# Reordering the opening of an encoder layer: memory keys in the large PSUM tiles, statistics spread later, x^T loads interleaved with weights

## The chip, the cores and the metric

The kernel runs on one core of a Trainium2 chip. The metric is the device time of one execution in microseconds (us). TensorE (PE) multiplies, VectorE (DVE), ScalarE (ACT) and GpSimd (POOL) work on tiles in SBUF or PSUM, and the queue of SyncE (SP) issues the DMA transfers of this kernel, one after another.

## The reference

One encoder layer is applied to two request groups with shared weights: a prompt of 1024 tokens and a sample of 512, each with 256 memory tokens, all of width 1024. Cut to what matters here:

```
h  = rms_norm(x, ln_pre);  z = h @ w_in            # projections and gates of three branches
kv = rms_norm(mem, ln_mem) @ w_mem_kv              # memory keys (512 wide) and values (512 wide)
pool, self-attention, cross-attention into mk/mv
merged = sum_n sigmoid(gate_n) * (branch_n @ w_branch[n])
y = x + rms_norm(merged @ w_out, ln_post)
```

The change touches only the opening: the norms of the memory and of the prompt, and the memory's keys and values.

## The kernel before, in words

Everything is float32 at the interface. A product is made of three float32r matmuls (`mm3`, lines 139 to 142, issued at L133): each operand is split into a high part (ACT copies with rounding, L172) and a low part (DVE subtracts, L169), and hi*hi + hi*lo + lo*hi is summed in PSUM. The split of a 128x1024 weight tile is in `weights` (lines 181 to 188). Weights use three raw buffers (`RAW`) and two split buffers (`WT`), so a third weight can be loaded only when a raw buffer is free, and split only when the matmuls of the weight two before it are done.

The opening is `mem_phase` (lines 661 to 723) with `long_h` (lines 237 to 286) run beside it: `mem_phase` calls `next(others)` at chosen points, and each call runs `long_h` up to its next `yield`.

`mem_phase` loads the memory transposed (`mt`, both groups side by side, 512 columns) in four pieces and the first two key weights, splits the memory with its gain (L675 on ACT, L676 on DVE), and then runs four key stages (c = 0 to 3, 24 matmuls each, one bank of 512 columns in a small PSUM tile `B`) and four value stages (kk = 0 to 3, 24 matmuls each, in the four banks of the two large PSUM tiles `A`). The memory's norm is applied to the keys when a bank is evacuated (L700, then a split into `hu` tiles and four DMAs to scratch, L705) and to the values as a per-partition scale (L719, L720).

A norm takes this path: squares on ACT (L209) and two adds on DVE (L210, L211), `mean_squares` (16 small matmuls against `ones`, two columns wide, then an ACT copy at L204), `rstd_of` on POOL (L192, L196), and `spread`: DVE makes four diagonal blocks (L218), one float32 matmul against `ones` turns them into a 128x512 tile of the factors. Before the change the memory's path stands behind key stage 0 and the spread ahead of key stage 1.

`long_h` does the same for x^T of the prompt, in two halves of tokens j = 0, 1: four loads of 1 MB each, then per half the norm, then `scaled` (L258) multiplies by gain and factor, and the differences (L266) and `put` (splits at L172 and L169) make seven operands h[0] to h[6] for `products`, which forms each pair of weight tiles with seven half-size products instead of eight. Product i needs h[i]. `products` follows on the value stages, so the first one starts when these are done and h[0] is ready.

The instruction order of every engine is fixed when the kernel is built: the framework's scheduler orders by readiness in its own model of time and by priority, which is program order, moved ahead by AHEAD = 120 for weight splits and by EVAC = 200 for evacuations. An engine then waits at an instruction until its inputs are there.

Of the kernel before, what the change touches and what calls it, by code (L numbers as in the profile page):

```python
# [13 lines left out]
AF = mybir.ActivationFunctionType  # L14
# [4 lines left out]
P = 128  # L19
# [42 lines left out]
def encoder_kernel(ctx: ExitStack, tc, wt, xs, xts, mt, cols, rows, rope, edge, ys):  # L62
# [34 lines left out]
    def S(n):  # L97
        return st.tile([P, n], F32, tag=f"s{n}", bufs=3 if n == 16 else 8, name=nm("s"))
# [46 lines left out]
    def load(out, src):  # L145
        return nc.sync.dma_start(out, src)
# [24 lines left out]
    def split(hi, lo, x):  # L171
        act.activation(hi, x, AF.Copy)  # L172
        lo_of(lo, x, hi)
# [4 lines left out]
    def SUM():  # L178
        return sb.tile([P, D], F32, tag="sum", bufs=2, name=nm("sum"))

    def weights(*key):

        raw = RAW()
        load(raw[:], wt[TILES[key]])
        hi, lo = WT()
        with tc.high_priority(AHEAD):
            split(hi[:], lo[:], raw[:])
        return lambda s: (hi[:, s], lo[:, s])

    def rstd_of(ss):  # L190

        pool.tensor_scalar(ss, ss, EPS, 1.0, op0=ALU.add, op1=ALU.mult)  # L192
        n = ss.free_size()
        for i in range(0, n, 4):
            j = slice(i, min(i + 4, n))
            pool.tensor_tensor(ss[:, j], ss[:, j], mhalf[:, :j.stop - i], op=ALU.pow)  # L196
# [40 lines left out]
    def long_h(xt, h):  # L237

        h += [[None] * 4 for _ in range(7)]
        xv = xt.rearrange("p (k t) -> p k t", k=KC)  # L240
        q = [[M(F32) for _ in range(2)] for _ in range(2)]
        for j in range(2):
            for i in range(2):
                load(q[i][j][:].rearrange("p (c n) -> p c n", c=4), xv[:, i * 4:i * 4 + 4, j * BLK:(j + 1) * BLK])
        yield
        r, sp = S(16), []
        for j in range(2):
            rj = r[:, j * TT:(j + 1) * TT]
            mean_squares([squares(q[i][j][:]) for i in range(2)], rj)
            rstd_of(rj)  # L250
            sp.append(spread(rj))
            yield
        b11, b12, b21, b22 = [[q[i][j][:, :D], q[i][j][:, D:]] for i in range(2) for j in range(2)]

        def scaled(i, j):
            for c in range(4):
                x = q[i][j][:, c * BLK:(c + 1) * BLK]
                v.scalar_tensor_tensor(x, x, colt[:, i * 4 + c:i * 4 + c + 1], sp[j], op0=ALU.mult, op1=ALU.mult)  # L258

        def put(k, x):  # L260
            for c in range(2):
                parts_of(h[k], 2 * c, x[c])

        def difference(out, a, b):
            for c in range(2):
                v.tensor_tensor(out[c], a[c], b[c], op=ALU.subtract)  # L266

        scaled(0, 0)
        put(0, b11)
        yield  # L270
        scaled(1, 0)
        put(1, b21)
        yield
        scaled(0, 1)
        scaled(1, 1)
        yield
        t3, t4 = (U(), U()), (U(), U())
        difference(t3, b22, b12)
        difference(b12, b12, b11)
        difference(b11, b22, b12)  # L280
        put(2, b11)
        put(3, b12)
        put(4, t3)
        put(5, b22)
        difference(t4, b21, b11)
        put(6, t4)
# [374 lines left out]
    def mem_phase(mkd, mvd, others):  # L661

        raw, mh, ml = [M(F32) for _ in range(2)], [], []
        ws = []
        for i in range(4):
            load(raw[i // 2][:, i % 2 * D:(i % 2 + 1) * D], mt[:, i * D:(i + 1) * D])
            if i < 2:
                ws.append(weights("mk", i))
        for i in range(4):
            x = raw[i // 2][:, i % 2 * D:(i % 2 + 1) * D]  # L670
            hi, lo = sb.tile([P, 1024], F32R, tag="kt", bufs=4, name=nm("mh")), U(F32R)
            for k in range(2):
                s = slice(k * BLK, (k + 1) * BLK)
                g = colt[:, 8 + 2 * i + k:9 + 2 * i + k]
                act.activation(hi[:, s], x[:, s], AF.Copy, scale=g)  # L675
                v.scalar_tensor_tensor(lo[:, s], x[:, s], g, hi[:, s].bitcast(F32), op0=ALU.mult, op1=ALU.subtract)  # L676
                mh.append(hi[:, s])
                ml.append(lo[:, s])
        next(others)
        yield  # L680
        m = list(zip(mh, ml))
        r, sp = S(16), HU()

        def rstd():
            mean_squares([squares(raw[i][:]) for i in range(2)], r[:, :TT])
            rstd_of(r[:, :TT])
            spread(r[:, :TT], sp[:])

        for c in range(4):
            b, w = B(), ws.pop(0) if ws else weights("mk", c)  # L690
            for k in range(KC):
                mm3(b[:], w(slice(k * P, (k + 1) * P)), m[k], k == 0, k == KC - 1)
            if c == 0:
                rstd()
            else:
                next(others, None)
            yield
            t, hi, lo = HU(), HU(F32R), HU(F32R)
            with tc.high_priority(EVAC):
                v.tensor_tensor(t[:], b[:], sp[:], op=ALU.mult)  # L700
                split(hi[:], lo[:], t[:])
            for g in range(2):
                for s, x in enumerate((hi, lo)):
                    o = s * D + c * NMEM
                    nc.sync.dma_start(mkd[g][:, o:o + NMEM], x[:, g * NMEM:(g + 1) * NMEM].bitcast(F32))  # L705
        b = [a[:, i * BLK:(i + 1) * BLK] for a in (A(), A()) for i in range(2)]
        for kk in range(4):
            w = weights("mv", kk)
            for i in range(2):
                k = kk * 2 + i  # L710
                for t in range(TT):
                    ts = slice(t * P, (t + 1) * P)
                    mm3(b[t], (m[k][0][:, ts], m[k][1][:, ts]), w(slice(i * 512, (i + 1) * 512)), k == 0, k == KC - 1)
            next(others, None)
            yield
        for t in range(TT):
            hi, lo = HU(F32R), HU(F32R)
            with tc.high_priority(EVAC):
                act.activation(hi[:], b[t], AF.Copy, scale=r[:, t:t + 1])  # L719
                v.scalar_tensor_tensor(lo[:], b[t], r[:, t:t + 1], hi[:].bitcast(F32), op0=ALU.mult, op1=ALU.subtract)  # L720
            for s, x in enumerate((hi, lo)):
                o = s * D + t % 2 * BLK
                nc.sync.dma_start(mvd[t // 2][:, o:o + BLK], x[:].bitcast(F32))
# [289 lines left out]
                nc.sync.dma_start(dst[t * P:(t + 1) * P, n], x[:, n])  # L1013


    load(colt[:], cols)
    v.tensor_scalar_mul(hbias[:], colt[:, 16:40], 0.5)
    mkd, mvd = [[scratch(f"{n}_{g}", [P, 2 * D]) for g in range(2)] for n in ("mk", "mv")]
    h, hs = [], []
    ops = long_h(xts[1], h)  # L1020
    run(mem_phase(mkd, mvd, ops))
    run(ops)
    late_constants()
    sc, kt, vt, pairs, bg, tasks, drained = group(1)
    pre = short_h(xts[0], hs)
# [114 lines left out]
```

## Time and profile before

| | us |
|---|---|
| median of 3 runs | 1512.16 (1507.26 to 1512.44) |
| the profiled execution, its own time | 1511.38 |
| its span, first to last instruction | 1509.6 |
| PE busy in the span | 1462.9 (97%) |
| DVE busy | 981.2 (65%) |
| ACT busy | 709.2 (47%) |
| mean granted TensorE clock | 0.99 of full |

The span is 1.8 us shorter than the profiled execution's time, which lies 0.8 us under the median. "Busy" is time in which an engine executes; the bracket at the end of a timeline row is the idle time of that engine just before it and what ended it.

### The profile page before, as it was taken

What the parts mean: (1) busy time and instruction counts of PE and PEld (TensorE: products, weight loads), DVE (VectorE), ACT (ScalarE), POOL (GpSimd) and SP (SyncE); (2) the same over time, 40 slices, a digit from 0 to 9 for tenths busy, and PEclk for the clock granted to TensorE, in tenths of its full rate; (3) what the DMA queues carried; (4) which work ended last, traced back from release to release, by engine and by line L of the source; (5) the groups of instructions that cost most, each with busy time, mean ns of one, the idle gap of its engine ahead of it and who ended that gap; (6) DMA issues with size and microseconds to landing.
All of it is one profiled execution on the core that took longest, in us unless ns stands there. A gap on an engine that the chain in (4) does not pass through costs nothing.

```text
span 1509.6 us, 19658 instructions
## 1 busy us (share of the span) xinstructions
PE 1462.9 (97%) x7264; PEld 1207.9 (80%) x7264; DVE 981.2 (65%) x1262; ACT 709.2 (47%) x1097; POOL 272.4 (18%) x286
## 2 busy tenths in 40 slices
PE   5999999999999999999999999999989999999998
PEld 3778888888888888887888888888767878888887
DVE  5896586666648564646676676666667664764754
ACT  5354444544434544434565555666666323323332
POOL 0001020110000000301222222233233150150241
PEclk8999999999999999999999999999999999999999
DMA  7333234332323433344322222265326854954952
GB/s 274 100 112 110 84 112 126 106 132 65 127 91 93 155 119 126 112 138 138 91 65 78 96 65 90 81 213 185 126 72 233 313 179 138 338 192 141 337 163 84
DMA packets 88174, 211.37 MB, mean 140 GB/s; under 512 B 9872, under 2 KB 19216, under 8 KB 87312
## 3 DMA queue, kind: packets, MB, share of 16 engines
q1 hardware_dynamic: 88080, 210.14, 42.1%
q8 instruction: 57, 0.93, 0.3%
q14 instruction: 37, 0.30, 0.1%
HBM read 155.57 MB, written 54.53 MB: 139 GB/s over the span
## 4 chain that ended last, share of the span: by engine, by line
PE 83%; issue 4%; ACT 4%; DVE 4%; DMA 2%; POOL 1%; SPq 0%; DVEq 0%; POOLq 0%; ACTq 0%
PE B L133 65%; PE A L133 13%; PE A L137 5%; ACT u L769 1%; DMA hu<-xq 1%; DVE wlo L169 1%; ACT med L172 1%; ACT whi L172 1%; DVE s L767 1%; PE B L137 1%; DMA hu<-merge 1%; POOL med L925 1%; POOL s L196 0%; DVE med L169 0%; DMA med<-q 0%
## 5 line engine op out<-in xcount | busy, mean ns | idle before, releaser
L133 PE MATMUL B<-med,whi 128*128 128x512 f32 x2776 | 870.3, 393 | 1.1 <-ACT hu L359 1.1
L133 PEld LDWEIGHTS B<-med,whi 128*128 128x128 f32 x2776 | 513.5, 188 | 104.5 <-ACT hu L359 2.3
L133 PE MATMUL B<-med,wlo 128*128 128x512 f32 x1388 | 542.6, 391 | 0.7 <-DVE wlo L169 0.7
L172 ACT ACTIVATE whi<-raw 128x1024 fp32r<-128x1024 f32 (+1 forms) x168 | 167.3, 996 | 304.4 <-PE B L133 212.6
L133 PEld LDWEIGHTS B<-med,wlo 128*128 128x128 f32 x1388 | 260.7, 188 | 55.9 <-DVE wlo L169 1.7
L169 DVE TENSOR_TENSOR wlo<-raw,whi 128x1024 fp32r<-128x1024 f32 (+1 forms) x168 | 213.0, 1268 | 139.3 <-ACT whi L172 136.8
L172 ACT ACTIVATE med<-A 128x1024 fp32r<-128x1024 f32 (+1 forms) x108 | 96.9, 897 | 121.3 <-PE A L137 121.1
L771 POOL TENSOR_SCALAR u<-u,s 128x1024 f32<-128x1024 f32 (+1 forms) x96 | 94.6, 985 | 317.0 <-DVE s L770 275.7
L169 DVE TENSOR_TENSOR med<-A,med 128x1024 fp32r<-128x1024 f32 (+1 forms) x109 | 115.7, 1061 | 51.6 <-ACT med L172 50.0
L767 DVE TENSOR_REDUCE s<-A 128x1 f32<-128x1024 f32 (+1 forms) x96 | 100.1, 1043 | 42.7 <-PE A L133 20.8
L192 POOL TENSOR_SCALAR s<-s 128x16 f32<-128x16 f32 (+3 forms) x17 | 6.6, 388 | 671.8 <-DVE s L557 324.6
L769 ACT ACTIVATE u<-A,s 128x1024 f32<-128x1024 f32 (+1 forms) x96 | 93.1, 970 | 46.3 <-DVE s L767 45.8
L137 PE MATMUL A<-ident,u 128*128 128x128 f32 x784 | 107.2, 275 | 4.6 <-DVE med L169 2.1
L137 PEld LDWEIGHTS A<-ident,u 128*128 128x128 f32 x784 | 90.8, 141 | 24.8 <-issue 9.6
L133 PE MATMUL A<-kt,med 128*128 128x512 f32 x320 | 96.5, 415 | 10.0 <-ACT u L769 8.8
L925 POOL TENSOR_TENSOR med<-med,hu 128x512 f32<-128x512 f32 x48 | 77.4, 1625 | 136.1 <-DVE hu L923 136.1
L133 PE MATMUL A<-whi,med 128*128 128x512 f32 (+1 forms) x320 | 92.4, 368 | 0.2 <-ACT hu L954 0.2
L172 ACT ACTIVATE whi<-sum 128x1024 fp32r<-128x1024 f32 x50 | 53.1, 1062 | 64.3 <-PE B L133 62.1
L133 PEld LDWEIGHTS A<-kt,med 128*128 128x128 f32 x320 | 54.4, 190 | 34.2 <-ACT u L769 22.9
L133 PE MATMUL B<-med,vt 128*128 128x256 f32 x512 | 76.1, 288 | 1.4 <-ACT med L172 1.4
L169 DVE TENSOR_TENSOR med<-med,med 128x1024 fp32r<-128x1024 f32 (+1 forms) x50 | 55.5, 1115 | 33.7 <-ACT med L172 29.9
L172 ACT ACTIVATE med<-med 128x1024 fp32r<-128x1024 f32 (+1 forms) x44 | 44.3, 1019 | 68.8 <-POOL med L925 42.6
(173 smaller groups left out, 1567.2 us busy)
## 6 DMA issues: line engine op xcount, KB each, us to landing
raw<-wt SPq DMA_DIRECT2D x168, 512.0 KB, 3.7
merge<-hu SPq DMA_DIRECT2D x72, 256.0 KB, 2.1
hu<-merge SPq DMA_DIRECT2D x72, 256.0 KB, 5.4
med<-br SPq DMA_DIRECT2D x36, 256.0 KB, 5.2
q<-hu SPq DMA_DIRECT2D x24, 256.0 KB, 2.6
br<-hu SPq DMA_DIRECT2D x24, 256.0 KB, 2.5
med<-q SPq DMA_DIRECT2D x12, 512.0 KB, 4.5
med<-xt_prompt SPq DMA_DIRECT2D x4, 1024.0 KB, 13.2
```

The costliest lines, as they stand in the source:

```text
L133: pe.matmul(out, l, r, **k)
L137: pe.transpose(out, x, i[:])
L169: v.tensor_tensor(out, x, hi.bitcast(F32), op=ALU.subtract)
L172: act.activation(hi, x, AF.Copy)
L192: pool.tensor_scalar(ss, ss, EPS, 1.0, op0=ALU.add, op1=ALU.mult)
L767: v.reduce_max(mx[:], a[:, :L], axis=AX.X, negate=True)
L769: act.activation(p[:, :L], a[:, :L], AF.Exp, bias=mx[:], accum_out=sm[:])
L771: pool.tensor_scalar(p[:, :L], p[:, :L], rc[:], 1.0, op0=ALU.mult, op1=ALU.mult)
L925: pool.tensor_tensor(at, at, sg[:], op=ALU.add)
```

## The change

It makes these edits, all in the opening:

- A first ACT instruction copies one column of a constant, so that the activation table is loaded there. The constants `colt` are loaded behind the first piece of the memory instead of ahead of it, and `hbias` is made from them after the opening instead of at the start.
- The first key weight is split in two halves.
- The x^T loads are issued one at a time, with the third and the fourth key weight between them.
- The four key stages write the four banks of two `A` tiles instead of four `B` tiles.
- The memory's mean squares come after key stage 1, its spread after key stage 2. Stages 0 to 2 are evacuated after that spread, stage 3 after its own matmuls. The squares of half 0 of x come after stage 2, its spread after stage 3, the squares of half 1 after value stage 0, its spread (with `scaled` and `put` for h[0]) after value stage 1. The differences come after the value stages.

```diff
-    def weights(*key):
+    def weights(*key, pieces=1):
...
         with tc.high_priority(AHEAD):
-            split(hi[:], lo[:], raw[:])
+            for i in range(pieces):
+                s = slice(i * D // pieces, (i + 1) * D // pieces)
+                split(hi[:, s], lo[:, s], raw[:, s])
...
                 load(q[i][j][:].rearrange("p (c n) -> p c n", c=4), xv[:, i * 4:i * 4 + 4, j * BLK:(j + 1) * BLK])
-        yield
+                yield
...
             rstd_of(rj)
+            yield
             sp.append(spread(rj))
-            yield
+            if j == 0:
+                yield
...
             load(raw[i // 2][:, i % 2 * D:(i % 2 + 1) * D], mt[:, i * D:(i + 1) * D])
+            if i == 0:
+                load(colt[:], cols)
             if i < 2:
-                ws.append(weights("mk", i))
+                ws.append(weights("mk", i, pieces=2 - i))
...
         next(others)
-        yield
+        ws.append(weights("mk", 2))
+        next(others)
+        ws.append(weights("mk", 3))
+        next(others)
+        next(others)
         m = list(zip(mh, ml))
         r, sp = S(16), HU()
-
-        def rstd():
-            mean_squares([squares(raw[i][:]) for i in range(2)], r[:, :TT])
-            rstd_of(r[:, :TT])
-            spread(r[:, :TT], sp[:])
-
-        for c in range(4):
-            b, w = B(), ws.pop(0) if ws else weights("mk", c)
-            for k in range(KC):
-                mm3(b[:], w(slice(k * P, (k + 1) * P)), m[k], k == 0, k == KC - 1)
-            if c == 0:
-                rstd()
-            else:
-                next(others, None)
-            yield
+        b = [a[:, i * BLK:(i + 1) * BLK] for a in (A(), A()) for i in range(2)]
+
+        def evacuate(c):
             t, hi, lo = HU(), HU(F32R), HU(F32R)
             with tc.high_priority(EVAC):
-                v.tensor_tensor(t[:], b[:], sp[:], op=ALU.mult)
+                v.tensor_tensor(t[:], b[c], sp[:], op=ALU.mult)
                 split(hi[:], lo[:], t[:])
...
+        for c in range(4):
+            for k in range(KC):
+                mm3(b[c], ws[c](slice(k * P, (k + 1) * P)), m[k], k == 0, k == KC - 1)
+            if c == 1:
+                mean_squares([squares(raw[i][:]) for i in range(2)], r[:, :TT])
+                rstd_of(r[:, :TT])
+            elif c == 2:
+                spread(r[:, :TT], sp[:])
+                for i in range(3):
+                    evacuate(i)
+                next(others)
+            elif c == 3:
+                next(others)
+                evacuate(3)
+            yield
...
-    load(colt[:], cols)
-    v.tensor_scalar_mul(hbias[:], colt[:, 16:40], 0.5)
+    act.activation(mhalf[:, :1], mhalf[:, 1:2], AF.Copy)
...
     run(mem_phase(mkd, mvd, ops))
     run(ops)
+    v.tensor_scalar_mul(hbias[:], colt[:, 16:40], 0.5)
```

## Rows read from the trace of the kernel before

**Rows 1.** Long stretches: us, busy of PE, PEld, DVE, ACT, POOL, clock, DMA share, GB/s.

```profile
0.00:90.00 90.00, 69.42 (x280) 54.17 (x281) 68.24 (x84) 43.57 (x48) 5.40 (x12) 0.89 0.55 185
90.00:110.00 20.00, 18.86 (x87) 14.42 (x86) 18.33 (x22) 10.78 (x15) 0.00 (x0) 1.00 0.26 81
110.00:200.00 90.00, 90.00 (x420) 74.08 (x419) 60.41 (x88) 37.23 (x55) 11.45 (x11) 1.00 0.27 86
```

**Rows 2.** The same view of the opening, cut at its stages.

```profile
7.50:17.20 9.70, 8.48 (x24) 5.87 (x24) 9.33 (x13) 9.70 (x12) 0.00 (x0) 1.00 1.04 399
17.20:21.40 4.20, 2.28 (x16) 2.14 (x16) 3.72 (x5) 3.80 (x3) 0.00 (x0) 0.94 1.05 387
21.40:28.60 7.20, 0.08 (x2) 0.04 (x1) 2.87 (x4) 4.31 (x4) 2.20 (x2) 0.50 0.91 325
28.60:37.80 9.20, 9.20 (x26) 6.75 (x27) 4.86 (x7) 1.63 (x3) 0.00 (x0) 0.68 0.27 95
...
42.20:51.50 9.30, 9.30 (x27) 6.74 (x28) 6.71 (x9) 2.12 (x2) 0.00 (x0) 0.68 0.36 86
...
62.30:82.40 20.10, 20.10 (x89) 16.53 (x88) 19.63 (x23) 6.89 (x8) 0.00 (x0) 1.00 0.44 127
82.40:104.00 21.60, 20.46 (x89) 15.85 (x89) 21.06 (x24) 15.15 (x19) 0.00 (x0) 1.00 0.35 126
sum 104.00, PE 82.28 PEld 63.74 DVE 81.89 ACT 51.12 POOL 5.40; mean PE 7.48 PEld 5.79 DVE 7.44 ACT 4.65 POOL 0.49
```

**Rows 3.** Timeline of PE, opening: start, us, line, what [idle before <-releaser].

```profile
28.56 2.08 PE L133 MATMUL B<-u,ones 128*128 128x512 f32 x2 [7.12 <-DVE u L218]
37.84 1.84 PE L133 MATMUL B<-ones,hu 128*128 128x2 f32 x16
42.20 2.04 PE L133 MATMUL B<-u,ones 128*128 128x512 f32 x2 [2.52 <-DVE u L218]
55.84 1.10 PE L133 MATMUL B<-u,ones 128*128 128x512 f32 x2 [0.30 <-DVE u L218]
```

**Rows 4.** Timeline of ACT, 0 to 38 us.

```profile
5.59 1.28 ACT L675 ACT_TABLE_LOAD   x1 [5.59 <-DMA med<-mt]
6.89 0.72 ACT L675 ACTIVATE mh<-med,colt 128x512 fp32r<-128x512 f32 x1
24.29 1.06 ACT L172 ACTIVATE whi<-raw 128x1024 fp32r<-128x1024 f32 x1 [3.29 <-DMA raw<-wt]
25.25 0.15 ACT L204 ACTIVATE s<-B 128x4 f32<-128x4 f32 x1
25.31 3.70 ACT L209 ACTIVATE med<-med 128x2048 f32<-128x2048 f32 x2
```

**Rows 5.** Timeline of DVE, opening.

```profile
7.64 0.75 DVE L676 SCALAR_TENSOR_TENSOR u<-med,colt,mh 128x512 fp32r<-128x512 f32 x1 [5.00 <-ACT mh L675]
27.81 0.69 DVE L218 TENSOR_TENSOR u<-ident,s 128x512 f32<-128x512 f32 x1 [1.21 <-POOL s L196]
44.28 2.72 DVE L258 SCALAR_TENSOR_TENSOR med<-med,colt,B 128x512 f32<-128x512 f32 x4 [1.02 <-PE B L133]
51.70 0.69 DVE L700 TENSOR_TENSOR hu<-B,hu 128x512 f32<-128x512 f32 x1 [1.76 <-PE B L133]
60.52 2.06 DVE L258 SCALAR_TENSOR_TENSOR med<-med,colt,B 128x512 f32<-128x512 f32 x3
102.14 1.22 DVE L169 TENSOR_TENSOR med<-u,med 128x1024 fp32r<-128x1024 f32 x1
```

**Rows 6.** Timeline of SP's queue: start, us of issuing, transfer.

```profile
0.72 0.39 SPq L146 DMA_DIRECT2D colt<-cols  x1
1.17 0.42 SPq L146 DMA_DIRECT2D med<-mt  x1
4.46 6.97 SPq L146 DMA_DIRECT2D med<-xt_prompt  x4
```

## The prediction

> **What bounds the kernel now.** I first read the busy time by long stretches: from 110 us on PE is busy without a gap, while the first 90 us hold 20.6 us without PE work and a mean granted clock of 0.89 [rows 1]. The change works only there, so its worth is read there: as much as it brings forward the moment from which PE runs without a gap.
>
> Then the same view cut at the stages [rows 2]. Key stage 0 takes 8.5 us of PE, because its memory operands come at the pace of ACT and DVE (both over 9.3 of 9.7 us busy). Then PE does almost nothing from 17.2 to 28.6. Key stages 1 and 2 (28.6 to 37.8 and 42.2 to 51.5) run at a mean granted clock of 0.68: after the gap the clock had been granted at 0.50, which is the 1.2 GHz level. The value stages show 24 matmuls at full clock: 20.1 us for some 88, so 0.228 us each and 5.5 us a stage.
>
> Third, what ends PE's gaps. Each of them ends with a spread: 7.12 us of idle time before the memory's, 2.52 before that of half 0 of x [rows 3]. The cause of the long one is on ACT: it stood 3.29 us at the split of the third key weight, whose DMA was queued behind 4 MB of x^T, and the copy of the memory's mean squares came after that, at 25.25 [rows 4]; from that copy to the spread the path over POOL and DVE took 3.3 us (28.56 - 25.25) [rows 3, 4].
>
> Last, DVE. Over the first 104 us it works 81.9, so 22.1 are idle; but from 62.3 to 104 it works 40.7 of 41.7 us [rows 2]. **In that stretch DVE is full too**: it makes the operands h[2] to h[6], and the last subtraction of h[6] ends at 103.4 (102.14 + 1.22) [rows 5], just as PE gets to the seventh product. So two engines have to be moved forward, and the later one sets the gain.
>
> **The change, step by step.**
>
> 1. *Start.* The table load (1.28 us) began only when the first piece of the memory had landed, at 5.59, and the first activation followed at 6.89 [rows 4]. With the load ahead of that, and the first piece issued at 0.72 instead of 1.17 [rows 6], the first L675 starts near 5.2 and DVE's first L676 near 6.0 instead of 7.64 [rows 5]. The gain is 1.6 us. `colt` now stands behind 0.5 MB: it lands with the piece (no cost, taken, since it is issued only one issue time later) or at worst with the next 0.5 MB, which at 399 GB/s [rows 2] is 1.3 us. The Trainium skill ("ScalarE: Activation LUTs", What ACT_TABLE_LOAD costs) gives a switch 1283 ns and a drain of some 1380 ns; the trace shows the first part and no drain, since the first activation starts 0.02 us after the load. By the page 1.4 us more would be gained. The two halves of the first weight let PE start about 0.4 us earlier and cost one more instruction on ACT and DVE, some 0.1 us each; `hbias` moves 0.2 us of DVE work to a fuller place. I take both as nothing.
>
> 2. *Key stages on PE.* Stage 0 starts near 7.0 and keeps its 8.5 us (its cover, ACT and DVE, is the bound): 15.4. Stage 1 has its weight and no spread ahead of it: 20.9. The 16 matmuls of the mean squares take 1.84 [rows 3]: 22.7. Stage 2 needs the third weight. It now stands behind 4.5 MB instead of 7; at about 395 GB/s that is some 6.5 us off the 24.3 at which ACT got it [rows 4], so 17 to 18, and its split buffer is free at 15.4. So stage 2 runs from 22.7 to 28.2, and the memory's 3.3 us path from mean squares to spread (26 us) lies under it. Spread 0.55 us (1.10 for two parts [rows 3]), the squares of half 0, stage 3: 36.1. No gap and no cold stretch is left here.
>
> 3. *x^T.* Its last two loads come behind 1 MB more, some 2.7 us later: the last lands at about 25. Its squares are wanted on PE only behind value stage 0 (42 us), so over 10 us of cover. The fourth weight's load waits in the SP queue for the first raw buffer, free near 9; x^T half 1, queued behind it, loses nothing, since issuing all of x^T took until 11.4 anyway [rows 6] and the transfers in flight outlast the wait.
>
> 4. *Added waits.* The value stages use the `A` tiles that the keys now hold, so the matmuls into the last two banks wait for the evacuations of stages 2 and 3. An evacuation reads its bank in 0.69 us (L700) [rows 5]; six matmuls into the first two banks (1.4 us) cover that of stage 3. Nothing is lost if the first three evacuations go under stage 3 (taken: they are issued from 29 on, and need 2 us); if the spread comes late, or the `hu` buffers (eight, of which an evacuation takes three until its DMAs are out) run short, all of it lies open: up to 4 us, and a cold restart of PE. That costs 3.1 us, by the 9.2 us that stage 1 with its spread took instead of 6.1 [rows 2].
>
> 5. *Value stages.* Spread of half 0 at 36.6, value stage 0 to 42.1, squares of half 1 to 44, value stage 1 to 49.5, spread 50.0, the rest to 61 instead of 82.4. **PE alone would gain 21 us.**
>
> 6. *DVE.* From 36.6 to 50 it has eight L258 (0.68 each [rows 5]: 5.4), four subtractions for h[0] and h[1] (1.14 each with overlap: 4.6), the last key evacuation (1.3) and one weight (1.1): 12.4 of 13.4 us. So it can start on half 1 when its spread comes, at 50.0; before, it got there at 60.52 [rows 5], being busy until then. From there its list is nearly the same, and it was full. **It gains 10.5 us**, and h[6] is ready at 92.9. Two items (2.4 us) that stood behind 60.5 are now done sooner; I set them against waits in DVE's fixed order, as the 1.76 before L700 [rows 5].
>
> So DVE sets the end: PE, ready for products at 61, makes two of them (h[0], h[1]) and then waits for h[2] to h[6]. The sum is 1511.4 (the profiled execution) less 10.5: **1501 us**. That execution lies 0.8 us under the median of the runs, which is no term.
>
> **Rivals.**
>
> - *DVE loses its idle time more fully.* Of the 22.1 us of idle time, some 6 before the first memory operand can't go, which leaves 16: 1495 us. For it: the list of step 6 leaves room before 50. Against: half 1 of x can't begin before its spread, which PE reaches at 50. Chance 0.10.
> - *The gain is partly given back.* Either the wait of step 4 lies open, or ACT or DVE again stands at something out of turn, as ACT did for 3.29 us, or PE's gaps in the first products bring the clock down. Each costs 3 to 7.5 us of the 10.5: 1504 to 1508 us. For it: PE waits some 8 us in the products, and the clock did fall after the gap of 7.12. Against: there, DVE sets the pace, and PE's slower matmuls hide in its waits except at the end. Chance 0.22.
> - *Slower: half 0 is held behind half 1.* In program order L258 for half 0 now stands behind the spread of half 1, after value stage 1. If DVE's fixed order keeps to that, DVE idles from 37 to near 52 and all operands slip by 15 us: h[6] at 107 instead of 103.4, PE waits over 10 us with h[0] and h[1] too, and comes back cold (2.9): 1511.4 + 3.6 + 2.9 = 1518 us. It decides from a first L258 later than some 48 us. Against: before, L258 ran at 44.28, within a microsecond of its spread, ahead of the evacuation of stage 2 (51.70) that precedes it in the program [rows 5]. Chance 0.06.
> - *The table load does not move,* because it is placed with the first activation that waits for data. Then 1.3 us of step 1 stay: 1502 us. Chance 0.02.
>
> The forecast keeps 0.60.
>
> **How the numbers follow.** About 0.5% (7.6 us of the median) is what a measurement of this kernel can tell from no change, so faster means under 1504.6. That is the forecast, the first rival and the last: 0.72. The second rival lies nearly all within 0.5%; with the milder half of the third that makes 0.24, and 0.04 are left for slower by more. The range runs from the first rival's 1495 to the second's 1508, which leaves out the slower case and the edges of the others, under 2 in 10.
>
> **What would show it.** Right: a table load near 1 us and a first L675 near 5.2; no PE gap over 1 us between key stages and one clock rise; value stages done near 61; DVE nearly full from 36 to 93; PE waiting for L169 or L266 in the first seven products; the first L258 near 37 and half 1 near 50; PE gapless from about 94. Wrong: a value stage that waits for L700, a first L258 behind 48, or PE gapless before 90 (then DVE is not the bound that I take it for).

## The result, and the profile after

The changed kernel takes 1516.26 us (median of 10 runs, 1513.77 to 1517.74); the kernel before, run beside it, takes 1511.7 (10 runs). The ratio is 1.004, 95% interval [1.0027, 1.0053], so 4 to 8 us more. The profiled execution took 1516.54 us, with a span of 1514.7, which is 5.1 more than before, and a mean granted clock of 0.987. The forecast was 1501, with 1508 as the upper end. That is under the 0.5% which the prediction takes for the least that can be told, but the whole interval lies above 1, so the change costs a little, where a gain was forecast.

**Where the time went.** The busy time by long stretches, kernel after (columns as in [rows 1]):

```profile
0.00:90.00 90.00, 63.79 (x270) 50.02 (x270) 63.87 (x82) 40.24 (x46) 5.61 (x12) 0.89 0.57 191
90.00:110.00 20.00, 18.23 (x67) 14.06 (x68) 18.68 (x20) 12.08 (x14) 0.00 (x0) 0.81 0.09 27
110.00:200.00 90.00, 90.00 (x426) 74.01 (x425) 58.98 (x84) 39.01 (x58) 8.65 (x9) 1.00 0.27 88
```

Against [rows 1], PE was busy 5.6 us less in the first 90 us (270 matmuls instead of 280), and from 90 to 110 it worked at a granted clock of 0.81 instead of 1.00, so it got through 67 matmuls there, not 87. From 110 on both are full: the loss lies ahead of that. PE's timeline shows it (kernel after, answering [rows 3]):

```profile
7.53 0.80 PE L133 MATMUL A<-mh,whi 128*128 128x512 f32 x1 [7.53 <-ACT whi L172]
27.73 1.72 PE L133 MATMUL B<-ones,hu 128*128 128x2 f32 x14 [0.98 <-DVE hu L213]
33.29 2.08 PE L133 MATMUL B<-u,ones 128*128 128x512 f32 x2 [3.84 <-DVE u L220]
38.86 0.77 PE L133 MATMUL A<-whi,mh 128*128 128x512 f32 x1 [3.49 <-DVE hu L698]
42.84 0.52 PE L133 MATMUL A<-mh,whi 128*128 128x512 f32 x1
50.32 1.02 PE L133 MATMUL B<-u,ones 128*128 128x512 f32 x2
62.17 1.02 PE L133 MATMUL B<-u,ones 128*128 128x512 f32 x2
74.03 0.61 PE L133 MATMUL B<-med,whi 128*128 128x512 f32 x2
90.49 0.79 PE L133 MATMUL B<-med,whi 128*128 128x512 f32 x1 [10.86 <-ACT med L172]
92.57 1.22 PE L133 MATMUL B<-med,whi 128*128 128x512 f32 x2 [1.29 <-ACT med L172]
```

The products of the kernel before begin here (answering 74.03):

```profile
82.44 0.62 PE L133 MATMUL B<-med,whi 128*128 128x512 f32 x2
```

Key stages 0 to 2 now run without a gap, from 7.53 to 26.5. Then come the memory's mean squares (27.73) and its spread, behind 3.84 us of waiting. Next in PE's order stands value stage 0, not key stage 3: it waits 3.49 us for a key evacuation (L698), does nine matmuls, and only then key stage 3 begins (42.84). The factors of half 0 are spread at 50.32, those of half 1 at 62.17 (steps 2 and 5 had 36.6 and 50.0; before it was 42.20 and 55.84 [rows 3]). The products start 8.4 us sooner than before, at 74.0 instead of 82.4, but after the two whose operands h[0] and h[1] exist, PE waits 10.86 + 1.29 us for h[2]. What was won ahead of the products is lost there, and more, and the clock with it. The stretches around that wait:

```profile
26.50:38.90 12.40, 4.09 (x20) 2.37 (x18) 9.69 (x12) 8.71 (x9) 2.11 (x2) 0.62 0.43 146
74.00:92.60 18.60, 6.45 (x27) 4.64 (x25) 18.27 (x21) 7.59 (x10) 0.00 (x0) 0.77 0.38 118
92.60:104.80 12.20, 12.20 (x43) 9.70 (x43) 10.88 (x12) 7.38 (x9) 0.00 (x0) 0.79 0.15 43
```

From 74.0 to 92.6 PE is busy for 6.45 us, DVE for 18.27 of 18.60: DVE is full and PE waits for it. The timeline of DVE, kernel after (answering [rows 5]):

```profile
17.51 1.23 DVE L169 TENSOR_TENSOR wlo<-raw,whi 128x1024 fp32r<-128x1024 f32 x1 [2.76 <-ACT whi L172]
22.05 1.23 DVE L169 TENSOR_TENSOR wlo<-raw,whi 128x1024 fp32r<-128x1024 f32 x1 [3.31 <-ACT whi L172]
42.07 0.68 DVE L213 TENSOR_TENSOR hu<-med 128x512 f32<-128x512 f32 x1
42.91 0.69 DVE L213 TENSOR_TENSOR hu<-med 128x512 f32<-128x512 f32 x1 [0.15 <-DMA mk<-hu]
48.98 0.69 DVE L220 TENSOR_TENSOR u<-ident,s 128x512 f32<-128x512 f32 x1 [5.38 <-POOL s L198]
54.32 2.06 DVE L262 SCALAR_TENSOR_TENSOR med<-med,colt,B 128x512 f32<-128x512 f32 x3
107.41 1.22 DVE L169 TENSOR_TENSOR med<-u,med 128x1024 fp32r<-128x1024 f32 x1
```

DVE idles 2.76 and 3.31 us at the low parts of the third and the fourth key weight. The last adds of the squares of half 0 (L213 at 42.07 and 42.91) stand behind three key evacuations. Then DVE idles 5.38 us at the diagonal blocks for the factors of half 0 (L220). The first L262 (L258 before) runs at 54.32 instead of 44.28, the last low part of h[6] ends at 108.6 instead of 103.4. Why the memory's statistics came late is on ACT (kernel after, answering [rows 4]):

```profile
0.72 1.28 ACT L1030 ACT_TABLE_LOAD   x1 [0.72 <-PEq L1144]
5.62 1.33 ACT L681 ACTIVATE mh<-med,colt 128x512 fp32r<-128x512 f32 x2 [3.41 <-DMA colt<-cols]
16.42 1.06 ACT L172 ACTIVATE whi<-raw 128x1024 fp32r<-128x1024 f32 x1 [2.70 <-DMA raw<-wt]
20.96 1.06 ACT L172 ACTIVATE whi<-raw 128x1024 fp32r<-128x1024 f32 x1 [3.48 <-PE A L133]
21.93 7.30 ACT L211 ACTIVATE med<-med 128x2048 f32<-128x2048 f32 x4
```

The splits of key weights 2 and 3 stand ahead of the memory's squares (L211). ACT waits 2.70 us for the weight's DMA and 3.48 us for the matmuls that hold the split buffer, with the squares, whose input had landed long before, queued behind it until 21.93.

**How much DVE lost.** DVE's work up to 104 us in two stretches, kernel before:

```profile
0.00:50.00 50.00, 29.71 (x102) 22.14 (x103) 31.30 (x42) 25.21 (x26) 4.15 (x10) 0.80 0.65 228
50.00:104.00 54.00, 52.56 (x234) 41.60 (x233) 50.59 (x58) 25.92 (x31) 1.25 (x2) 1.00 0.38 117
```

and after:

```profile
0.00:50.00 50.00, 34.16 (x138) 26.65 (x139) 27.05 (x37) 25.48 (x28) 4.01 (x10) 0.86 0.69 249
50.00:104.00 54.00, 41.85 (x175) 32.91 (x174) 49.49 (x58) 23.87 (x29) 1.60 (x2) 0.87 0.32 94
```

PE is ahead by 4.5 us of busy time at 50 (138 matmuls against 102), DVE behind by 4.25. Up to 104 DVE did 5.35 us less (76.54 against 81.89), and the span grew by 5.1. One moment behind the first products serves as a **mark** below: ACT's first copy of the prompt's values into `vt` (L580, L576 before), at 107.46 before and 112.75 after. It moved by 5.3 us, the same amount.

### The profile page after: what moved, and what is told of

It reads as the page before. It is cut to its first block, busy times and chain, and to the rows that moved or that the text cites. A ratio compares the mean times of both kernels' runs of the same rounds, so it can differ in the third digit from the quotient of the medians.

```text
span 1514.7 us, 19662 instructions
## 1 busy us (share of the span) xinstructions
PE 1462.4 (97%) x7264; PEld 1207.5 (80%) x7264; DVE 980.2 (65%) x1263; ACT 709.9 (47%) x1099; POOL 273.1 (18%) x286
## 4 chain that ended last, share of the span: by engine, by line
PE 80%; issue 5%; DVE 5%; DMA 4%; ACT 4%; POOL 1%; SPq 0%; DVEq 0%; POOLq 0%; ACTq 0%
PE B L133 61%; PE A L133 13%; PE A L137 5%; ACT u L783 1%; DVE wlo L169 1%; DMA hu<-xq 1%; DVE s L781 1%; DMA hu<-merge 1%; ACT med L172 1%; PE B L137 1%; ACT whi L172 1%; DMA med<-br 1%; DVE med L169 0%; DMA u<-rows 0%; POOL med L939 0%
```

## The experiments

Three theories. **P**: PE's own gaps ahead of 43 us are the loss. **H6**: as predicted, DVE's whole list up to h[6] sets the end. **H2**: what counts is when PE can go on behind products 0 and 1, that is when h[2] is ready; what DVE does for h[5] and h[6] is covered. If H2 holds, DVE's idle time ahead of h[2] and its order count, and nothing behind. The expectations of e1 to e4 speak of a theory D, which H6 and H2 later split: DVE and the time at which half 0 of x gets its factors decide.

P falls by the traces already shown. PE's gaps ahead of 43 us did not keep it from reaching the products 8.4 us sooner than before, and the kernel is slower all the same. g1, below, says it again from the other side.

The times, each against runs of the kernel before on the same chip; "DVE" is its busy time from 0 to 50 us:

| run | median us | ratio [95%] | PE goes on at | DVE | mark |
|---|---|---|---|---|---|
| before | | 1 | no such wait | 31.30 | 107.46 |
| after | 1516.26 | 1.0040 [1.0027, 1.0053] | 92.57 | 27.05 | 112.75 |
| e1 | 1515.96 | 1.0038 [1.0026, 1.0049] | 93.67 | 26.94 | 113.59 |
| e2 | 1517.41 | 1.0048 [1.0031, 1.0065] | 92.39 | 27.03 | 111.54 |
| e3 | 1513.27 | 1.0015 [1.0004, 1.0025] | 90.75 | 26.51 | 111.24 |
| e4 | 1511.01 | 1.0000 [0.9987, 1.0014] | 87.07 | 29.85 | 107.65 |
| d1 | 1514.00 | 1.0019 [1.0008, 1.0030] | 94.54 | 26.49 | 113.11 |
| e5 | 1513.55 | 1.0023 [1.0011, 1.0034] | 90.01 | 27.13 | 111.66 |
| f1 | 1515.03 | 1.0027 [1.0017, 1.0038] | 88.99 | 26.60 | 112.85 |
| e6 | 1508.10 | 0.9983 [0.9973, 0.9994] | 82.10 | 31.67 | 105.99 |
| f2 | 1508.48 | 0.9986 [0.9976, 0.9996] | 82.38 | 31.97 | 107.10 |
| g1 | 1508.78 | 0.9983 [0.9973, 0.9993] | no such wait | 31.31 | 107.23 |
| p1 | 1510.47 | 1.0003 [0.9992, 1.0013] | no such wait | 31.47 | 106.53 |
| p2 | 1511.24 | 1.0005 [0.9995, 1.0016] | no such wait | 30.26 | 108.72 |
| e7 | 1516.02 | 1.0039 [1.0024, 1.0053] | 85.21 | 31.17 | 110.28 |
| e8 | 1516.21 | 1.0038 [1.0024, 1.0053] | 85.38 | 31.30 | 110.45 |

The last three columns are of one execution each and the medians of nine or more. Single executions differ in the long rest too (the profiled one of e2 has a span of 1511.3, far under its median), so the ratios give the verdicts and the traces the places.

### e1: the evacuations of key stages 2 and 3 both behind stage 3

```diff
             elif c == 2:
                 spread(r[:, :TT], sp[:])
-                for i in range(3):
+                for i in range(2):
                     evacuate(i)
                 next(others)
             elif c == 3:
                 next(others)
+                evacuate(2)
                 evacuate(3)
```

> Edit of the changed kernel: stages 0 and 1 are evacuated after the spread, stages 2 and 3 after stage 3, so that stage 3 no longer stands behind the reading of the bank beside it in the same A tile. Theory D (DVE and the time at which half 0 of x gets its factors decide; PE has 10.9 us to spare at 79.6 us): PE's waits before 38.9 us shrink by some 6 us, but half 0's squares still wait for hu buffers, so h[6] moves little and the time falls by 0 to 3 us, to 1513 to 1516. Theory P (PE's waits and its cold stretch from 33 to 43 us are the loss): 5 us or more are gained, 1511 or less.

No change in the time, but the edit did not do to PE what was expected of it. PE's gaps of the kernel with this edit, and its first product:

```profile
36.89 2.07 PE L133 MATMUL B<-u,ones 128*128 128x512 f32 x2 [2.78 <-DVE u L220]
42.57 0.77 PE L133 MATMUL A<-whi,mh 128*128 128x512 f32 x1 [3.61 <-DVE hu L698]
75.73 0.62 PE L133 MATMUL B<-med,whi 128*128 128x512 f32 x2
91.59 0.79 PE L133 MATMUL B<-med,whi 128*128 128x512 f32 x1 [10.26 <-ACT med L172]
```

Key stage 3 now runs ahead of the memory's spread, which comes 3.6 us later (36.89). The waits of 3.84 and 3.49 us became 2.78 and 3.61, where "some 6 us" less were expected, and PE ran at a granted clock of 0.50 from 42.6 to 52. It reaches the products 1.7 us later than after does (75.73 against 74.03). By 90 us PE is busy 67.42 us instead of 63.79, but for the same 270 matmuls: the difference is slower work, not more of it. So e1 gave PE no lead and doesn't test theory P; by itself it only shows that this edit is worth nothing.

### e2: the memory's squares ahead of the splits of key weights 2 and 3

```diff
         next(others)
+        with tc.high_priority(AHEAD):
+            sq = [squares(raw[i][:]) for i in range(2)]
         ws.append(weights("mk", 2))
...
             if c == 1:
-                mean_squares([squares(raw[i][:]) for i in range(2)], r[:, :TT])
+                mean_squares(sq, r[:, :TT])
```

> Edit of the changed kernel: the memory's squares and adds are issued ahead of the splits of key weights 2 and 3 on ACT and DVE. Theory D: ACT's and DVE's waits between 14 and 22 us are filled, the memory's spread comes 4 to 6 us earlier than 33.3, half 0's factors 3 to 5 us earlier, and the time falls by 3 to 5 us, to 1511 to 1513. Theory P: the wait for the spread (3.8 us) goes, the wait of stage 3 for the evacuation of stage 2 stays: 2 to 4 us. The place of the first L262 tells them apart: under D the time follows it.

Alone it brought nothing. The mean squares came much earlier, but PE's order now had them inside key stage 0 (a gap of 1.56 us there). The spread stayed where it was in that order, at 34.82, half 0's spread came at 50.42 as after, and the first L262 at 54.44. The memory's diagonal blocks (DVE) and its spread (PE) in this kernel:

```profile
22.18 0.69 DVE L220 TENSOR_TENSOR u<-ident,s 128x512 f32<-128x512 f32 x1 [3.22 <-POOL s L198]
34.82 1.02 PE L133 MATMUL B<-u,ones 128*128 128x512 f32 x2
```

The blocks were ready 12 us ahead of the spread, so what held it is PE's order. ACT's waits at the two weight splits did not go either (3.02 and 2.68 us, in after 2.70 and 3.48). So the place of the memory's squares is not the only thing that holds the factors of half 0.

### e3: the last add of the squares in place, without a `hu` buffer

```diff
-        sq, a = M(F32), HU()
+        sq = M(F32)
...
-        v.tensor_tensor(a[:], sq[:, :BLK], sq[:, BLK:D], op=ALU.add)
-        return a
+        v.tensor_tensor(sq[:, :BLK], sq[:, :BLK], sq[:, BLK:D], op=ALU.add)
+        return sq
```

> Edit of the changed kernel: the last add of the squares writes into its own med tile instead of a hu tile, so that the norms of x don't wait for hu buffers held by the key evacuations. Theory D: half 0's last add moves from 42 us to near 30, its mean squares and its spread come before value stage 0, the first L262 near 45 instead of 54.3, and the time falls by 5 to 8 us, to 1508 to 1511. Theory P: PE's waits for the memory's spread and for the evacuation of stage 2 (3.8 and 3.5 us) stay, and the time falls by 1 us at most.

Some 3 to 4 us less than after (1513.27; 1.0015 against 1.0040, and the intervals just miss each other), where theory D expected 5 to 8. DVE's timeline of this kernel:

```profile
37.70 0.68 DVE L213 TENSOR_TENSOR med<-med 128x512 f32<-128x512 f32 x1
41.88 0.69 DVE L220 TENSOR_TENSOR u<-ident,s 128x512 f32<-128x512 f32 x1 [2.89 <-POOL s L198]
49.51 0.69 DVE L220 TENSOR_TENSOR u<-ident,s 128x512 f32<-128x512 f32 x1 [5.14 <-POOL s L198]
50.12 0.74 DVE L262 SCALAR_TENSOR_TENSOR med<-med,colt,B 128x512 f32<-128x512 f32 x1
```

The add that ran at 42.91 now runs at 37.70, and half 0's spread starts at 42.62 instead of 50.32: the `hu` buffers, held by the key evacuations, had kept the adds back. (Little of that is an open wait in the trace of the kernel after, 0.15 us for a DMA out of a `hu` tile; the rest is DVE's order, built with the buffers taken. In g1 below the same edit stands in the kernel before, and half 0's spread comes no earlier there, so before the change these buffers did not hold it.) But a new wait took most of it. DVE's order has the diagonal blocks of half 1 (L220) ahead of the first L262 of half 0, and DVE stood there for 5.14 us although the factors of half 0 were there by some 44.7 (42.62 + 2.07). That is the mechanism of the rival on the slower side.

### e4: e1, e2 and e3 together

> The three edits together: stage 2 evacuated after stage 3, the memory's squares ahead of the splits, the last add in place. Theory D: first L262 near 38 to 42 us, h[6] at 97 to 101 instead of 108.6, time down by 8 to 12 us, 1504 to 1508, faster than the kernel before. Theory P: PE's gaps before 43 us go, 6 to 8 us, but nothing beyond.

The time is that of before, 1.0000: as far as the interval can tell, the three places together make the whole loss. Alone, e1 and e2 bring nothing and e3 a part. It is not the gain on the kernel before that theory D expected (1504 to 1508). The spread of half 0 comes at 44.02, DVE does 29.85 us of work by 50 instead of 27.05, PE goes on at 87.07. PE reaches its wait for h[2] 4.7 us sooner than after does (74.95 against 79.63) and stands there nearly as long (10.03 and 1.28 us), so h[2] itself is 5.5 us sooner. DVE's work up to 104 us goes with the times here: 76.54 us after, 77.68 in e3, 81.16 in e4, 81.89 before. Its work up to 50 alone doesn't: e3 has 26.51, less than after, and is faster. Here too DVE waits 3.53 us for POOL at the blocks of half 1 ahead of its first L262 (51.48).

### d1: work for h[5] and h[6] left out

```diff
-    def parts_of(h, c, x):
+    def parts_of(h, c, x, lo=True):
...
-        split(tv[:, :, 0], tv[:, :, 1], x.rearrange("p (c n) -> p c n", c=2))
+        xr = x.rearrange("p (c n) -> p c n", c=2)
+        if lo:
+            split(tv[:, :, 0], tv[:, :, 1], xr)
+        else:
+            act.activation(tv[:, :, 0], xr, AF.Copy)
...
-                parts_of(h[k], 2 * c, x[c])
+                parts_of(h[k], 2 * c, x[c], k < 5)
...
-        difference(t4, b21, b11)
-        put(6, t4)
+        put(6, t3)
```

> The changed kernel with DVE work left out behind h[2]: the four low parts of h[5] and h[6] are not made (the high part stands in for them) and h[6]'s difference is not formed (h[4]'s operand stands in). That is six instructions of 1.14 us, 6.8 us of DVE work, with PE's matmuls unchanged. Theory H6 (the end of DVE's full stretch, h[6] at 108.6 us, sets the time): 5 to 7 us less, 1509 to 1511. Theory H2 (the time at which PE may go on after products 0 and 1, 92.6 us, sets it; from there PE runs at its own pace): only the one difference that stood ahead of h[2]'s low part counts, 0 to 1.5 us less, 1514.5 to 1516.

This is the kernel after without six instructions of DVE at the end of the opening (6.8 us). By the ratios 3 us were gained (1.0040 to 1.0019), with intervals that overlap a little, so the gain may be anything from near nothing to some 6. This execution reached its first matmul 0.9 us later than after did; less that, its mark moved by 0.5 us. PE's waits:

```profile
88.35 0.45 PE L137 MATMUL A<-ident,u 128*128 128x128 f32 x1 [7.06 <-DVE u L424]
92.75 0.79 PE L133 MATMUL B<-med,whi 128*128 128x512 f32 x1 [3.95 <-ACT med L172]
94.54 0.79 PE L133 MATMUL B<-med,whi 128*128 128x512 f32 x1 [0.99 <-DVE med L169]
```

PE waits for h[2] just as long. H6 wanted 5 to 7 us and a time of 1509 to 1511, H2 at most 1.5 us: the measured 3 us (1514.0) lie between them. Work behind h[2] counts, for about half of its length as far as these runs can tell, so neither theory holds as stated.

### e5: the differences for h[2] first

```diff
-        t3, t4 = (U(), U()), (U(), U())
-        difference(t3, b22, b12)
-        difference(b12, b12, b11)
-        difference(b11, b22, b12)
+        n12, t4 = (U(), U()), (U(), U())
+        difference(n12, b12, b11)
+        difference(b11, b22, n12)
         put(2, b11)
-        put(3, b12)
-        put(4, t3)
+        difference(b12, b22, b12)
+        put(3, n12)
+        put(4, b12)
```

> Edit of the changed kernel: the same differences in another order. b12 - b11 goes to the u tiles, h[2] is formed from it at once, and the difference for h[4] is formed afterwards, in place. DVE's work is the same, h[2] is ready two instructions (2.3 us) earlier. Theory H2: 2 to 3 us less, 1513 to 1514.5. Theory H6: no change, 1516.

PE goes on 2.6 us earlier (90.01), waits 1.45 us more in the next products, and the median falls by 2.7 us to 1513.55. The intervals of e5 and after overlap, and the mark moved by 1.1.

### f1: e5, with the scaling and `put` of h[0] to h[2] moved ahead

```diff
-        scaled(0, 1)
-        scaled(1, 1)
+        with tc.high_priority(AHEAD):
+            scaled(0, 1)
+            scaled(1, 1)
...
+        with tc.high_priority(AHEAD):
+            difference(n12, b12, b11)
+            difference(b11, b22, n12)
+            put(2, b11)
```

(and the same around `scaled(0, 0)`, `put(0, b11)`, `scaled(1, 0)` and `put(1, b21)`)

> The changed kernel with the new order of the differences and with scaled and put of h[0] to h[2] moved ahead, but without the three edits that take idle time out of the keys. Theory (the time at which PE goes on behind products 0 and 1 sets the time, and DVE's order and its idle time ahead of that are separate terms): the factors of half 0 still come near 50, PE goes on at 87 to 90 instead of 82.1, the time is 1510 to 1513. If DVE's order is all that counts, the time is that of the best version so far, 1508 plus or minus 1. If the order brings nothing while the factors are late, it is that of the order of the differences alone, 1513.5 plus or minus 1.

PE went on at 88.99, inside the stated range, but the time, 1515.03, is 2 us above it. The trace shows why: behind the wait for h[2] come further ones, and PE's waits in the products add up to 11.0 us against 12.15 after.

```profile
86.91 0.79 PE L133 MATMUL B<-med,whi 128*128 128x512 f32 x1 [6.43 <-ACT med L172]
88.99 1.22 PE L133 MATMUL B<-med,whi 128*128 128x512 f32 x2 [1.29 <-ACT med L172]
95.26 0.73 PE L133 MATMUL B<-med,whi 128*128 128x512 f32 x2 [1.63 <-ACT med L172]
```

H2 doesn't hold as stated here either. With h[2] early, the next operands are late, so DVE's list behind h[2] counts too, as in d1. How far down the list, no run shows.

### e6: e4 with f1's order

No new edit.

> The three edits of e4 (stage 2 evacuated after stage 3, squares first, last add in place), the differences in the order of e5, and L262 and the operands h[0] to h[2] ahead of other DVE work by priority. Theory H2: PE goes on after products 0 and 1 at 81 to 83 us instead of e4's 87.1, with a gap of 3 to 6 us instead of 10: 1504 to 1507. Theory H6: as e4, 1511.

1508.1 us, ratio 0.9983 [0.9973, 0.9994]: faster than both kernels, by 2.6 us against before. That is 1 us above H2's range and 3 under H6's figure. The first L262 comes at 46.62, DVE has done 31.67 us by 50 and 82.97 by 104, PE goes on at 82.10. PE's first product and its first waits in the products:

```profile
68.74 0.62 PE L133 MATMUL B<-med,whi 128*128 128x512 f32 x2
80.02 0.80 PE L133 MATMUL B<-med,whi 128*128 128x512 f32 x1 [5.65 <-ACT med L172]
82.10 1.22 PE L133 MATMUL B<-med,whi 128*128 128x512 f32 x2 [1.29 <-ACT med L172]
```
With after, e4 and f1 this makes a square. The three edits against idle time bring 0.0040 without the new order (after to e4) and 0.0044 with it (f1 to e6), some 6.0 and 6.6 us. The order brings 0.0013 without them (after to f1) and 0.0017 with them (e4 to e6), some 2.0 and 2.6 us. The first pair is far outside the intervals; the second is within them each time, though both agree.

### f2: e6 with the squares of x moved ahead

```diff
-            mean_squares([squares(q[i][j][:]) for i in range(2)], rj)
+            with tc.high_priority(AHEAD + 100):
+                sq = [squares(q[i][j][:]) for i in range(2)]
+            mean_squares(sq, rj)
```

> The best version so far with the squares of both halves of x moved ahead on ACT and DVE, and all differences on DVE. If the factors of half 1 are what DVE still waits for, its scaling of half 1 begins 2 to 3 us earlier and the time falls to 1505 to 1507. If DVE is full from the factors of half 0 on, the squares only change places with other work of DVE: 1508 plus or minus 1.

No change from e6 (1508.48 and 1508.1). The spread of half 1 did not come earlier (67.27 and 66.96); DVE's work changed places.

### g1: the kernel before with the start, the loads, the in-place add and f1's order

No new edit; the keys stay in the four `B` tiles, and the statistics behind the stages where they were.

> The kernel before (key stages in B tiles, each spread and evacuated as before) with the table load first, the interleaved loads, the last add of the squares in place, and the differences in e5's order at e6's priority. Both theories: ACT no longer stands at the third key weight, PE's gap of 7.1 us ahead of the memory's spread shrinks to 3 to 4 us, half 0's factors come some 5 us earlier than 44.3. H2: 1503 to 1507. H6: 1505 to 1508.

1508.78 us, ratio 0.9983, the same as e6. PE reaches the products here:

```profile
83.95 0.62 PE L133 MATMUL B<-med,whi 128*128 128x512 f32 x2
```

That is 15.2 us later than e6 (68.74), and then PE has no wait there; e6 gives its lead back in waits of 10.25 us and at a granted clock of 0.91 from 82 to 104. So PE's lead is worth nothing by itself, and the `A` tiles and the later statistics, even with the three delays removed, are worth nothing that these runs can tell.

What both theories expected on the way did not come: the memory's spread starts at 28.77 and half 0's at 42.45, where they were before (28.56 and 42.20 [rows 3]). The time is just above both ranges, and the mark is 0.2 us earlier. So the trace of this one execution, the slowest of g1's ten, doesn't show where the 2.6 us come from. Which of g1's parts brings them was not tried.

### p1 and p2: the start alone, the loads alone

p1 is the kernel before with the table load, `colt`, `hbias` and the halves of the first weight as changed; p2 is the kernel before with the x^T loads in turns with the weights.

> The kernel before with the start of the change alone: table load first, colt behind the first piece of the memory, the first key weight split in halves, hbias later. Theory W (what is won at the start is lost at the next wait, here ACT's wait for the third key weight, whose DMA ends when it did): 0 to 0.5 us less, 1510 to 1511. Theory S (it adds up, as step 1 of the prediction has it): 1.6 us less, 1509.

> The kernel before with the interleaved loads alone (third and fourth key weights between the x^T loads). The third weight lands some 6 us earlier. If that wait was the cause of PE's gap of 7.1 us, the memory's spread comes 3 us or more before 28.6, half 0's factors near 41, and the time falls by 2 to 4 us, 1507 to 1508.5. If the splits of the two weights now stand ahead of the squares on ACT, as in the changed kernel, the squares wait for key stage 0 and the gain is under 1 us.

Neither moves the time. The memory's spread on PE, p1:

```profile
28.63 2.08 PE L133 MATMUL B<-u,ones 128*128 128x512 f32 x2 [6.61 <-DVE u L220]
```

and p2:

```profile
29.91 2.08 PE L133 MATMUL B<-u,ones 128*128 128x512 f32 x2 [2.40 <-DVE u L218]
```

In p1 PE starts 1.1 us sooner than before (7.54 against 8.61), but the memory's spread comes at 28.63, where it was before (28.56 [rows 3]), since the split of the third key weight still ends ACT's wait. The mark is 0.9 us earlier, less than the runs resolve. In p2 the third weight is there sooner (ACT splits it at 17.60), but its split waits for the split buffer with the memory's squares behind it, the same trap as in the kernel after, and the spread is 1.35 us later than before.

### e7 and e8: differences on POOL

e7 is e6 with the differences for h[4] and h[6] on POOL, e8 is e7 with the squares of x as in f2.

```diff
-        def difference(out, a, b):
+        def difference(out, a, b, on=v):
...
-                v.tensor_tensor(out[c], a[c], b[c], op=ALU.subtract)
+                on.tensor_tensor(out[c], a[c], b[c], op=ALU.subtract)
...
-        difference(b12, b22, b12)
+        difference(b12, b22, b12, pool)
...
-        difference(t4, b21, b11)
+        difference(t4, b21, b11, pool)
```

> e6 with the differences for h[4] and h[6] (four instructions of 1.14 us on DVE) on POOL, which is idle there. If DVE's work sets the pace of h[3] to h[6] in e6 (PE waits of 1.6, 0.8, 0.4 and 0.5 us behind h[2]): 2 to 4 us less than e6, 1504 to 1506. If POOL is slower at it than the products can wait (3 us each): no change or slower, 1508 to 1510.

> e7 with the squares of x also ahead of the weight splits by priority, since ACT stood idle at splits for 3.0 and 3.1 us before 30 us in e6. If DVE's idle time before half 0's factors counts one to one: 2 to 3 us less than e7, 1501 to 1504. If half 0's factors wait for PE's order and not for the squares: as e7.

Both lose what e6 had won, and more than either branch of the expectation of e7 had. POOL's timeline and DVE's groups of lines from 76 to 106 us (busy, mean ns of one), e7:

```profile
77.39 9.99 POOL L270 TENSOR_TENSOR med<-med,med 128x1024 f32<-128x1024 f32 x2 [26.48 <-DVE u L270]
87.34 6.63 POOL L270 TENSOR_TENSOR u<-med,med 128x1024 f32<-128x1024 f32 x2
```

```profile
L169 DVE TENSOR_TENSOR med<-med,med 128x1024 fp32r<-128x1024 f32 x6 | 10.8, 1840 | 0.0
L169 DVE TENSOR_TENSOR wlo<-sum,whi 128x1024 fp32r<-128x1024 f32 x2 | 4.6, 2309 | 0.0
```

and the first of these groups in e6, in the same stretch:

```profile
L169 DVE TENSOR_TENSOR med<-med,med 128x1024 fp32r<-128x1024 f32 x6 | 7.1, 1219 | 0.0
```

Four differences moved off DVE save it 4.9 us (4 x 1.22), but while POOL works on them, DVE's own subtractions take 1840 and 2309 ns instead of 1219. Six of the first group alone cost 3.7 us more, and PE's longest wait behind h[2] (4.74 us, until 95.11) ends with a low part that DVE made beside POOL's work in 3.35 us.

## Why the prediction was wrong, step by step

**What held.** The reading of what bounds the opening held (though not every gap of PE's ends with a spread: two short ones, 0.51 and 1.48 us, end with adds of the memory's squares). DVE is full behind the factors, PE waits for DVE's operands in the products, and a lead of PE's own is worth nothing (after against before, and g1 against e6). Step 1's sizes held: table load at 0.72, first L681 at 5.62 (5.2 predicted), first L682 at 6.38 (6.0), first matmul at 7.53 (7.0). `colt` cost a little, as the first L681 waited for it last. `hbias` did not move: DVE still made it at the start, at 5.56, as soon as `colt` had landed. The activation behind the moved table load starts at 2.01, 0.01 us after the load ends. The Trainium skill ("ScalarE: Activation LUTs", What ACT_TABLE_LOAD costs) gives every switch to another table set a drain beside the load. Behind this first load the trace shows none, and neither does that of before. But step 1 was a term that could not count by itself (p1).

**Step 2 failed first.** It said that the memory's path of 3.3 us would lie under key stage 2, with the spread ready at 26. PE's part of it held (the third weight was split at 16.42 and key stage 2 ended at 26.5), and so did the length of the path (30.08 to 33.29). But it followed PE and never placed the squares on ACT. ACT kept to its order, with two weight splits (program order less AHEAD) ahead of the squares, and waited 2.70 us at the third weight for its DMA and 3.48 at the fourth for its split buffer; so the path began late, and the spread came at 33.29. The prediction had seen that very trap in the kernel before (3.29 us at the third weight) and took it as removed, while the change only put a shorter DMA wait and a new buffer wait in its place. Putting this right alone brings nothing (e2), as PE's order then holds the spread.

**Step 4 failed next.** Its risk was seen and its price was taken as nothing. The value stages do wait for an evacuation of the keys (3.49 us), key stage 3 falls behind them, and the `hu` buffers run short. That last part is the only one whose removal gains by itself (e3), and it costs not on PE, where step 4 looked for it. It holds back the last adds of half 0 to 42.91, and by e3 some 7.7 us of half 0's factors (50.32 less 42.62). Step 4's own price, "up to 4 us, and a cold restart of PE", was of the right size for PE (3.84 and 3.49, at a mean granted clock of 0.62 from 26.5 to 38.9), but PE reached the products 8.4 us early all the same, so PE's share doesn't count.

**Steps 5 and 6** inherited this, and step 6 carries the one term of the sum, 10.5 us gained on DVE: by 104 us DVE had done 5.35 us less than before. Half 0's factors were spread at 50.3 instead of 36.6, half 1's at 62.2 instead of 50.0. DVE was to be full from 36.6 on; it idled 5.38 us ahead of 48.98 and had done 4.25 us less than before by 50. Even with all three delays removed (e6) DVE did only 31.67 us by 50, just 0.4 more than before. So the 10.5 us were not just blocked: step 6 moved DVE's whole list forward by as much as half 1's spread was to come sooner, and did not ask whether DVE's idle time ahead of 50, 18.7 us before, would go. In e6 it is still 18.3: some 5.7 lie ahead of the first memory operand, and 8.5 are three waits, 3.54 for POOL's factors, 1.98 and 2.94 for ACT's splits. Whether an order exists that takes it lower was not found.

**The rivals.** The one on the slower side gave 1518 us (its cold restart is 2.9 us, where step 4 has 3.1, and 92.9 with a slip of 15 is 107.9, not 107), by a first L258 behind 48, a wait over 10 us with h[0] and h[1] done, and a cold restart. All three happened (54.32, 12.15 and a granted clock of 0.79), and the time is near it, but by luck. Its cause was another: half 0 was late by its own factors. Only when these came earlier (e3, e4) did DVE's order hold half 0 behind half 1. The argument against it, that L258 ran promptly in the kernel before, was about an order that the change rebuilds. "Gain partly given back" named the right mishaps (an engine at something out of turn, the open wait of step 4, the clock) but let them eat into a gain that did not exist. The table load did move, and DVE's idle time did not shrink.

**The part that stays open.** The three edits of e4 were not tried in pairs, so how they share the 6 us is open. So is how far down DVE's list a late operand still costs (d1 and f1), and what makes g1 faster than before.

## What to carry to other kernels

When a change brings one engine forward, list what each of the other in-order engines has queued ahead of the wanted instruction, and for each entry which DMA or which buffer it waits for; a weight split that the scheduler moves ahead can stand at a full buffer with ready work behind it. A shared buffer that also carries statistics, as `hu` here, ties a critical path to the drain of unrelated stores; writing in place took it off. And where the bound engine's idle time is to shrink, name each of its present waits and what removes it, since moving its last input forward doesn't remove them. To see whether PE got ahead, compare the time of one and the same matmul, or the count: busy time also grows when the clock falls (e1).

## What the runs showed of the hardware that was not expected

Subtractions of 128x1024 on DVE and POOL at the same time can slow each other down. On DVE alone one takes 1.22 us (e6). Beside POOL's in e7, the group means rise to 1.84 and 2.31 us; one by one, those that start at 82.36, 85.08, 88.38 and 91.70 take 2.79 to 3.40 us. But the three of DVE from 78.36 to 81.8, beside POOL's first, kept their 1.2 us, and that one took POOL 6.68 us, its other three 3.3 each. (POOL's spans are rough in this profile.) What they contend for, no run here shows.
